# Transformer layer on one core: the MLP's norm factor stays in its PSUM bank and is applied in two portions, small evacuations are given priority, and the conv mixer's norm is spread over more steps

## The chip, the cores and the metric

The kernel runs on one core of a Trainium2 chip. The metric is the device time of one launch in microseconds; the median of the timed runs counts. A core has TensorE (PE, with its weight loads shown apart as PEld), VectorE (DVE), ScalarE (ACT), GpSimd (POOL) and the DMA queues, most of them issued here by SyncE (SP). Each engine works through its own instructions in the order in which the program puts them, and waits for others by semaphores.

## What is computed

One layer of a streaming encoder on x (2048 tokens, width 1024), all in float32:

```python
h = _rmsnorm(x, g_attn)
p = h @ w_in
y_a = a_b * _causal_dwconv(a_c * a_h, w_conv_a)
g = b_glu[..., :CONV_B_WIDTH] * jax.nn.sigmoid(b_glu[..., CONV_B_WIDTH:])
g = _causal_dwconv(g, w_conv_b) + b_conv_b
y_b = jax.nn.silu(_layernorm(g, ln_b_g, ln_b_b))
o = _stick_breaking(heads(q), heads(k), heads(v))
x = x + jnp.concatenate([y_a, y_b, y_c], axis=-1) @ w_out
h2 = _rmsnorm(x, g_ffn)
x = x + jnp.square(jax.nn.relu(h2 @ w_ff1)) @ w_ff2
```

`y_c` is o with its heads put side by side; a last RMS norm follows. The second convolution has 31 taps per channel, the attention has 8 heads of 64 and weighs a key by the product of the later keys' complements (no softmax), and the MLP has 4096 inner units.

## The kernel before

**Data.** Tokens lie along the free dimension in four blocks of 512 (`tb` = 0 to 3), channels on the 128 partitions, so a 128x512 tile is 128 channels of one block. Each factor of a large product is split into a high and a low part, and `mm3` (lines 100 to 108) does it as three passes of matmuls: high weights by high data (L103), low weights by high data (L105), high weights by low data (L107). The split of a tile is an ACT copy for the high part (L88) and a subtraction for the low one (L90, on DVE or POOL).

**Stages.** In the trace, the start and the input norms run to about 120 us; the input projection in two halves to about 512 us, each half with the conv mixer of two token blocks and, in the second half, the first round of the attention woven in; then come four blocks, which begin at about 512, 1000, 1500 and 2000 us. A block is the output projection, then the MLP, with the attention of the next token block woven in.

**The conv mixer** (`mixer_b`). For each token block and each of two channel groups, 31 DVE steps (L450, L452) add up the taps in a PSUM bank that bears the tag "c", of which there is one; an ACT copy takes the result to SBUF (`cb0`, `cb1`, L456). Then comes the LayerNorm over channels: the mean by two matmuls (L459, `ps_mean`, into the same single bank), its subtraction on DVE (L462), squares on ACT (L464), their sum on POOL (L467), a column sum on PE (L127, `ps_ss`), the reciprocal root (L115 on DVE, L118 on POOL), its spread over the partitions by PE (L134, `ps_R`), and the product. Each `yield` is a place where the weave can go over to other work; its number is a cost, and the number beside the mixer where it is woven in (83 and 98) is the cost that is spread over the half.

**The MLP of a block** (`block`). `acc0` to `acc7` hold the block's residual stream in SBUF. `ffn1(c)` makes 128 inner units in 24 matmuls, in two halves of 12; its bank `ps_u` goes through Relu and Square on ACT (L917, L918), is copied as high part `fh` (L926, ACT), and DVE subtracts for the low part `fl` (L927). After four such units `ffn2` multiplies them by the second weights into `ps_y`, and DVE adds that to acc (L952). After `ffn1(2)` the residual is multiplied by a factor of the norm: `mt` per token (L967), spread over the partitions by eight small matmuls into `ps_R` (L134), copied by ACT into an SBUF tile `ms` (L973), and then eight DVE multiplications acc = acc * ms (L975). The `z` banks (three in this stage) that `spread` takes from are also those of the attention's scores `ps_z` (L518, L519).

**The order of the work.** A scheduler puts each engine's instructions in order, by priorities that follow the order in which the program is written, and by a simulated time line. `high_priority(offset=HP)`, with HP = 200, moves the instructions inside it ahead by that many places in priority. The semaphores then keep that order on each engine.

Of the kernel before, what the change touches and what calls it, by code (L numbers as in the profile page):

```python
# [7 lines left out]
F32 = mybir.dt.float32  # L8
F32R = mybir.dt.float32r
# [6 lines left out]
P = 128  # L16
# [3 lines left out]
TB = 512  # L20
# [14 lines left out]
def f(ap):  # L35
    return ap.bitcast(F32)
# [32 lines left out]
class Trunk:  # L69
# [371 lines left out]
    def mixer_b(self, hf):  # L441
        nc = self.nc
        for tb in (2 * hf, 2 * hf + 1):
            acc = []
            for c in range(2):
                while (c, tb) not in self.g:
                    yield None
                g = self.g[c, tb]
                t = self.psum("ps_c", "c")
                nc.vector.tensor_scalar(t, g[:, 0:TB], self.wb[:, c, 0:1], self.vb["b_conv_b"][:, c : c + 1], op0=ALU.mult, op1=ALU.add)  # L450
                for k in range(1, 31):
                    nc.vector.scalar_tensor_tensor(t, g[:, k : k + TB], self.wb[:, c, k : k + 1], t, op0=ALU.mult, op1=ALU.add)  # L452
# [3 lines left out]
                nc.scalar.activation(acc[c], t, AF.Copy)  # L456
            mean = self.psum("ps_mean", "c")
            for c in range(2):
                nc.tensor.matmul(mean, self.avg, acc[c], start=c == 0, stop=c == 1)  # L459
            sqs = []  # L460
            for c in range(2):
                nc.vector.tensor_tensor(acc[c], acc[c], mean, op=ALU.subtract)  # L462
# [4 lines left out]
            nc.gpsimd.tensor_tensor(sqs[0], sqs[0], sqs[1], op=ALU.add)  # L467
            yv = self.rsqrt(self.colsum(sqs[:1], "c"), 1.0 / 256.0, LN_EPS)
            for _ in range(4):
                yield 1.8  # L470
            R = self.spread(yv, "c")
            for c in range(2):
                gg, bb = self.vb["ln_b_g"][:, c : c + 1], self.vb["ln_b_b"][:, c : c + 1]
                nc.vector.tensor_tensor(acc[c], acc[c], R, op=ALU.mult)
                s = self.mx.tile([P, TB], F32, name="sq", tag="sq", bufs=2)
                nc.scalar.activation(s, acc[c], AF.Sigmoid, bias=bb, scale=gg)
                nc.scalar.activation(acc[c], acc[c], AF.Identity, bias=bb, scale=gg)
                nc.gpsimd.tensor_tensor(s, acc[c], s, op=ALU.mult)

                nc.gpsimd.dma_start(self.Y[256 + c * P : 256 + (c + 1) * P, tb * TB : (tb + 1) * TB], s)  # L480
                yield 1.8
# [342 lines left out]
    def block(self, tb, before):  # L824
# [76 lines left out]
        def ffn1(*cs):  # L901

            for c in cs:
                need1(c)
            if len(cs) == 1:
                need1(cs[0] + 1)
            ws = [w1.pop(c) for c in cs]
            pus = [self.psum("ps_u", "d") for _ in cs]
            for q in range(2):
                for w, ps in zip(ws, pus):  # L910
                    self.mm3(ps, [(*w(d), hh[d], hl[d]) for d in range(4 * q, 4 * q + 4)], start=q == 0, stop=q == 1)
                    if q == 0:
                        yield 2.6
            if len(cs) > 1:
                need1(cs[-1] + 1)
            for c, ps in zip(cs, pus):
                nc.scalar.activation(ps, ps, AF.Relu)  # L917
                nc.scalar.activation(ps, ps, AF.Square)  # L918
                if tb == 3 and c > FC - G:

                    hi = self.at.tile([P, TB], F32R, name="fh", tag="Ahi", bufs=self.ab["Ahi"])
                    lo = self.at.tile([P, TB], F32R, name="fl", tag="Alo", bufs=self.ab["Alo"])
                else:
                    hi = hp.tile([P, TB], F32R, name="fh", tag="fh", bufs=G + 1)
                    lo = hp.tile([P, TB], F32R, name="fl", tag="fl", bufs=G + 1)
                nc.scalar.activation(hi, ps, AF.Copy)  # L926
                nc.vector.tensor_tensor(lo, ps, f(hi), op=ALU.subtract)  # L927
                fh[c], fl[c] = hi, lo
            yield 2.6 * len(cs)

        def ffn2(g, cols=slice(0, TB), ahead=0, again=0):

            cs = range(g * G, (g + 1) * G)

            def items(d):
                n = 4 * (g + again) + d // 2
                need2(n)
                t = w2[n]
                return [(t[:, 0, c % G, d % 2], t[:, 1, c % G, d % 2], fh[c][:, cols], fl[c][:, cols]) for c in cs]

            begun = []
            for d in range(ahead):
                begun.append(self.psum("ps_y", "d")[:, cols])
                self.mm3(begun[d], items(d)[:-1], stop=False)
            for d in range(DC):
                if d < ahead:
                    ps = begun[d]
                    self.mm3(ps, items(d)[-1:], start=False)
                else:
                    ps = self.psum("ps_y", "d")[:, cols]  # L950
                    self.mm3(ps, items(d))
                nc.vector.tensor_tensor(acc[d][:, cols], acc[d][:, cols], ps, op=ALU.add)  # L952
# [16 lines left out]
        nc.vector.scalar_tensor_tensor(em, mt, RMS_EPS, mt, op0=ALU.mult, op1=ALU.mult)  # L969
        yield from ffn1(2)  # L970
        need2(2)
        ms = hp.tile([P, TB], F32, name="ms", tag="ss", bufs=2)
        nc.scalar.activation(ms, self.spread(mt, "z"), AF.Copy)  # L973
        for d in range(DC):
            nc.vector.tensor_tensor(acc[d], acc[d], ms, op=ALU.mult)  # L975
        ss2 = hp.tile([P, TB], F32, name="ss2", tag="ss", bufs=2)
        sq7 = []
        for c in range(3, FC):
            yield from ffn1(c)
            if c < w2b:  # L980
                need2(c)
            if c % G == 0 and not (tb == 3 and c == FC - G):
                yield from ffn2(c // G - 1)
# [41 lines left out]
    def build(self):  # L1025
        tc = self.tc
        with ExitStack() as ctx:
# [6 lines left out]
            with ExitStack() as c1:  # L1034
                self.psum_pool(c1, d=3, c=1, z=2, q=1, o=1)
                self.p_pools(c1)
                self.w_eng = "dve"
                self.sb = 2
                self.xl = [[None] * DC for _ in range(2)]
                self.xh = [[None] * DC for _ in range(2)]  # L1040
                with tc.tile_pool(name="raw0", bufs=1) as self.rp:
                    self.rb, self.rt = 21, "raw"
                    self.p_start()
                self.rp = self.raw
                self.rb, self.rt = self.xb, "xt"
# [74 lines left out]
```

## Time and profile before

| | us |
|---|---|
| timed runs | 2442.66, 2449.86, 2449.74; median 2449.74 |
| profiled execution | 2452.1, of which the span is 2450.4 |
| mean granted TensorE clock, share of full speed | 0.992 |
| PE busy | 2390.6 |
| DVE busy | 1620.1 |
| POOL busy | 1161.3 |
| ACT busy | 1040.6 |

Times in the profile count from the start of the span; busy is the time in which an engine had an instruction in work. A row of a timeline gives start, duration, engine, line, operation, tiles and shape, a count if like instructions follow each other, and in brackets the idle time ahead of it with what ended it. PE's matmuls overlap, so a start-to-start distance says more of its pace than a duration.

### The profile page before, as it was taken

The page shows a single profiled execution, that of the slowest core. Times are in us where ns is not written, and L with a number is a line of the kernel's source. Part 1 is how long each engine was busy: PE and PEld are TensorE (multiplying, and loading weights), DVE is VectorE, ACT ScalarE, POOL GpSimd, SP SyncE. Part 2 cuts the span into 40 slices and gives each one's busy share as a digit, 9 for nine tenths or more (in the row PEclk, how much of TensorE's full clock was granted, in tenths as well). Part 3 has the DMA queues.
Part 4 walks back from the last instruction along what each step waited for, and adds up shares of the span by engine and source line. Part 5 has one row for each costly group of instructions (what it writes and reads, how often), then busy time and mean ns, then how long its engine had stood idle before and what let it go on. Part 6 is the DMA issues. An engine that isn't in the chain of part 4 may idle for free.

```text
span 2450.4 us, 32556 instructions
## 1 busy us (share of the span) xinstructions
PE 2390.6 (98%) x11316; PEld 2012.8 (82%) x11316; DVE 1620.1 (66%) x2380; ACT 1040.6 (42%) x1910; POOL 1161.3 (47%) x1221
## 2 busy tenths in 40 slices
PE   8999998999899999998999999999999999999998
PEld 7889877898788878887888888888888888888887
DVE  7957799943898977857777778577667735212114
ACT  5232532333466556534555555345555532121121
POOL 0342577641676666524676666168878720000000
PEclk9999999999999999999999999999999999999999
DMA  7569976779688777786877776876666556655555
GB/s 260 192 244 350 300 247 219 243 258 273 166 232 238 215 220 199 198 287 225 239 253 230 230 217 213 273 219 186 196 188 190 184 180 209 238 194 188 200 182 190
DMA packets 237061, 549.06 MB, mean 224 GB/s; under 512 B 26720, under 2 KB 100448, under 8 KB 218464
## 3 DMA queue, kind: packets, MB, share of 16 engines
q1 hardware_dynamic: 180304, 480.89, 58.1%
q0 software_dynamic: 37504, 56.64, 10.9%
q10 hardware_dynamic: 19088, 9.44, 1.3%
q8 instruction: 90, 1.47, 0.2%
q14 instruction: 75, 0.61, 0.1%
HBM read 390.38 MB, written 148.11 MB: 220 GB/s over the span
## 4 chain that ended last, share of the span: by engine, by line
PE 76%; DVE 15%; DMA 5%; issue 2%; POOL 1%; ACT 1%; SPq 0%; DVEq 0%; POOLq 0%; ACTq 0%
PE ps_y L107 8%; PE ps_y L103 8%; PE ps_y L105 8%; PE ps_u L103 7%; PE ps_u L105 7%; PE ps_u L107 7%; PE ps_p L105 4%; PE ps_p L107 4%; PE ps_p L103 4%; DVE A L659 2%; PE ps_x L103 2%; PE ps_z L518 2%; PE ps_x L105 2%; PE ps_x L107 2%; PE ps_z L519 2%
## 5 line engine op out<-in xcount | busy, mean ns | idle before, releaser
L90 POOL TENSOR_TENSOR Alo<-A,Ahi 128x512 fp32r<-128x512 f32 x288 | 395.1, 1383 | 104.2 <-PE ps_o L706 52.3
L952 DVE TENSOR_TENSOR acc<-acc,ps_y 128x512 f32<-128x512 f32 (+1 forms) x264 | 175.4, 667 | 195.6 <-PE ps_y L107 193.9
L107 PE MATMUL ps_y<-fl,w 128*128 128x512 f32 (+1 forms) x1056 | 279.8, 385 | 14.7 <-DVE fl L927 14.7
L103 PE MATMUL ps_u<-hh,w 128*128 128x512 f32 x1024 | 279.0, 393 | 6.2 <-DMA w<-s_w 6.2
L103 PE MATMUL ps_y<-fh,w 128*128 128x512 f32 (+1 forms) x1056 | 281.4, 386 | 2.5 <-DVE acc L952 1.3
L105 PE MATMUL ps_y<-fh,w 128*128 128x512 f32 (+1 forms) x1056 | 278.9, 384 | 0.0
L105 PE MATMUL ps_u<-hh,w 128*128 128x512 f32 x1024 | 275.0, 390 | 0.6 <-DVE w L90 0.6
L107 PE MATMUL ps_u<-hl,w 128*128 128x512 f32 x1024 | 275.0, 389 | 0.0
L601 POOL TENSOR_TENSOR A<-A,R 128x512 f32<-128x512 f32 x168 | 227.7, 1357 | 76.7 <-ACT A L599 54.6
L118 POOL TENSOR_TENSOR rs_y<-rs_v,mhalf 128x4 f32<-128x4 f32 (+1 forms) x13 | 14.7, 1131 | 523.3 <-DVE rs_v L117 486.1
L107 PEld LDWEIGHTS ps_y<-fl,w 128*128 128x128 f32 x1056 | 195.8, 189 | 55.9 <-DVE fl L927 17.0
L917 ACT ACTIVATE ps_u<-ps_u 128x512 f32<-128x512 f32 x128 | 74.8, 585 | 378.8 <-PE ps_u L107 378.5
L105 PEld LDWEIGHTS ps_y<-fh,w 128*128 128x128 f32 x1056 | 196.0, 189 | 40.2 <-DMA w<-wraw 0.4
L103 PEld LDWEIGHTS ps_y<-fh,w 128*128 128x128 f32 x1056 | 194.3, 189 | 40.7 <-DVE acc L952 2.1
L88 ACT ACTIVATE Ahi<-A 128x512 fp32r<-128x512 f32 x288 | 177.3, 627 | 118.4 <-PE ps_o L705 58.0
L105 PEld LDWEIGHTS ps_u<-hh,w 128*128 128x128 f32 x1024 | 192.1, 188 | 42.4 <-DVE w L90 1.5
L107 PEld LDWEIGHTS ps_u<-hl,w 128*128 128x128 f32 x1024 | 192.1, 188 | 40.1
L927 DVE TENSOR_TENSOR fl<-ps_u,fh 128x512 fp32r<-128x512 f32 x128 | 87.5, 685 | 207.1 <-ACT fh L926 206.6
L103 PEld LDWEIGHTS ps_u<-hh,w 128*128 128x128 f32 x1024 | 187.4, 189 | 42.5 <-DMA w<-s_w 6.4
L603 DVE TENSOR_TENSOR R<-ps_z,R 128x512 f32<-128x512 f32 x168 | 115.6, 688 | 126.4 <-ACT ps_z L600 93.8
L452 DVE SCALAR_TENSOR_TENSOR ps_c<-g,wb,ps_c 128x512 f32<-128x512 f32 x240 | 179.6, 748 | 4.6
L90 DVE TENSOR_TENSOR w<-wraw,w 128x512 fp32r<-128x512 f32 x152 | 150.4, 1007 | 24.1 <-ACT w L88 23.8
(175 smaller groups left out, 4881.2 us busy)
## 6 DMA issues: line engine op xcount, KB each, us to landing
w<-s_w SPq DMA_DIRECT2D x200, 512.0 KB, 3.4
w<-s_w SPq DMA_DIRECT2D x68, 1024.0 KB, 4.8
wraw<-in_w SPq DMA_DIRECT2D x192, 256.0 KB, 4.7
w<-s_w_out SPq DMA_DIRECT2D x64, 512.0 KB, 5.0
s_w<-w SPq DMA_DIRECT2D x32, 1024.0 KB, 5.4
s_w<-w SPq DMA_DIRECT2D x56, 512.0 KB, 4.4
Qd<-KQ SPq DMA_DIRECT2D x64, 256.0 KB, 6.4
xraw<-in_xT SPq DMA_DIRECT2D x48, 256.0 KB, 5.0
```

The source lines that it names most:

```text
L88: nc.scalar.activation(hi, x, AF.Copy)
L90: e.tensor_tensor(lo, x, f(hi), op=ALU.subtract)
L103: self.nc.tensor.matmul(ps, wh, xh, start=start and k == 0, stop=False)
L105: self.nc.tensor.matmul(ps, wl, xh, start=False, stop=False)
L107: self.nc.tensor.matmul(ps, wh, xl, start=False, stop=stop and k == n - 1)
L452: nc.vector.scalar_tensor_tensor(t, g[:, k : k + TB], self.wb[:, c, k : k + 1], t, op0=ALU.mult, op1=ALU.add)
L518: nc.tensor.matmul(z[:, oc], keys, g["qh"][:, qc], start=k == 0, stop=False)
L601: nc.gpsimd.tensor_tensor(t, t, R, op=ALU.mult)
L603: nc.vector.tensor_tensor(Rn, z, R, op=ALU.mult)
L917: nc.scalar.activation(ps, ps, AF.Relu)
L927: nc.vector.tensor_tensor(lo, ps, f(hi), op=ALU.subtract)
L952: nc.vector.tensor_tensor(acc[d][:, cols], acc[d][:, cols], ps, op=ALU.add)
```

## The change

It has four parts. The factor `ms` stays in the PSUM bank into which it was spread, with no ACT copy, and the eight multiplications read it from there. They are written in two portions of four with `ffn1(3)` between them. The evacuation of the inner units (Relu, Square, `fh`, `fl`) and the additions of `ps_y` to acc are put at high priority. And the mixer's norm is given three more yields ahead of the mean and two more ahead of the root, with larger costs for the weave (83 becomes 115, 98 becomes 116).

```diff
                 acc.append(self.mx.tile([P, TB], F32, name=f"cb{c}", tag="cb", bufs=2))
                 nc.scalar.activation(acc[c], t, AF.Copy)
+            for _ in range(3):
+                yield 1.8
             mean = self.psum("ps_mean", "c")
...
             yield 1.8
             nc.gpsimd.tensor_tensor(sqs[0], sqs[0], sqs[1], op=ALU.add)
+            for _ in range(2):
+                yield 1.8
             yv = self.rsqrt(self.colsum(sqs[:1], "c"), 1.0 / 256.0, LN_EPS)
...
-            for c, ps in zip(cs, pus):
-                nc.scalar.activation(ps, ps, AF.Relu)
-                nc.scalar.activation(ps, ps, AF.Square)
...
+            with self.tc.high_priority(offset=HP):
+                for c, ps in zip(cs, pus):
+                    nc.scalar.activation(ps, ps, AF.Relu)
+                    nc.scalar.activation(ps, ps, AF.Square)
...
+                    nc.scalar.activation(hi, ps, AF.Copy)
+                    nc.vector.tensor_tensor(lo, ps, f(hi), op=ALU.subtract)
+                    fh[c], fl[c] = hi, lo
...
-                nc.vector.tensor_tensor(acc[d][:, cols], acc[d][:, cols], ps, op=ALU.add)
+                with self.tc.high_priority(offset=HP):
+                    nc.vector.tensor_tensor(acc[d][:, cols], acc[d][:, cols], ps, op=ALU.add)
...
-        ms = hp.tile([P, TB], F32, name="ms", tag="ss", bufs=2)
-        nc.scalar.activation(ms, self.spread(mt, "z"), AF.Copy)
+        ms = self.spread(mt, "z")
         for d in range(DC):
+            if d == DC // 2:
+                yield from ffn1(3)
             nc.vector.tensor_tensor(acc[d], acc[d], ms, op=ALU.mult)
...
-        for c in range(3, FC):
+        for c in range(4, FC):
...
-                weave(self.p_half(0), [(Side(self.mixer_b(0)), 83, 20, 225, True), (Side(self.x_norms()), 24, 60, 180, True)])
+                weave(self.p_half(0), [(Side(self.mixer_b(0)), 115, 20, 225, True), (Side(self.x_norms()), 24, 60, 180, True)])
...
-                weave(self.p_half(1), [(Side(self.mixer_b(1)), 98, 0, 200, True), (a0, 28, 0, 210, True), (Side(self.pre_split()), len(self.presplit), 0, 200, True)])
+                weave(self.p_half(1), [(Side(self.mixer_b(1)), 116, 0, 200, True), (a0, 28, 0, 210, True), (Side(self.pre_split()), len(self.presplit), 0, 200, True)])
```

**What the scheduler makes of it.** A row below is one instruction: line, operation, output<-inputs and shape; a number behind a name tells one buffer from another of that name. Lines of the kernel after are 2 to 7 higher than those of the same code before (L975 is L982, L927 is L932, L459 is L461). SP's order is the same from the first block on, and PE's is the same from the middle of the second block on; in the third and fourth block only the ACT copy is gone.

DVE in the first block, before: the `fl` of one inner unit, the eight multiplications, a running sum of the attention (`R`), the low part of a first weight (`w1`), the next `fl`.

```order
L927 TENSOR_TENSOR fl_5993<-ps_u_5956,fh_5992 128x512
L975 TENSOR_TENSOR acc0_5546<-acc0_5546,ms_6015 128x512
L975 TENSOR_TENSOR acc1_5553<-acc1_5553,ms_6015 128x512
L975 TENSOR_TENSOR acc2_5562<-acc2_5562,ms_6015 128x512
L975 TENSOR_TENSOR acc3_5602<-acc3_5602,ms_6015 128x512
L975 TENSOR_TENSOR acc4_5642<-acc4_5642,ms_6015 128x512
L975 TENSOR_TENSOR acc5_5682<-acc5_5682,ms_6015 128x512
L975 TENSOR_TENSOR acc6_5722<-acc6_5722,ms_6015 128x512
L975 TENSOR_TENSOR acc7_5758<-acc7_5758,ms_6015 128x512
L603 TENSOR_TENSOR R_6063<-ps_z_6056,R_6003 128x512
L90 TENSOR_TENSOR w1_6132<-wraw_6133,w1_6132 128x512
L927 TENSOR_TENSOR fl_6080<-ps_u_6043,fh_6079 128x512
```

DVE at the same place, after:

```order
L932 TENSOR_TENSOR fl_5993<-ps_u_5956,fh_5992 128x512
L982 TENSOR_TENSOR acc0_5546<-acc0_5546,ps_R_6015 128x512
L982 TENSOR_TENSOR acc1_5553<-acc1_5553,ps_R_6015 128x512
L982 TENSOR_TENSOR acc2_5562<-acc2_5562,ps_R_6015 128x512
L982 TENSOR_TENSOR acc3_5602<-acc3_5602,ps_R_6015 128x512
L982 TENSOR_TENSOR acc4_5642<-acc4_5642,ps_R_6015 128x512
L982 TENSOR_TENSOR acc5_5682<-acc5_5682,ps_R_6015 128x512
L982 TENSOR_TENSOR acc6_5722<-acc6_5722,ps_R_6015 128x512
L982 TENSOR_TENSOR acc7_5758<-acc7_5758,ps_R_6015 128x512
L607 TENSOR_TENSOR R_6056<-ps_z_6049,R_6003 128x512
L90 TENSOR_TENSOR w1_6130<-wraw_6131,w1_6130 128x512
L932 TENSOR_TENSOR fl_6073<-ps_u_6036,fh_6072 128x512
```

The eight stand where they stood, all together and ahead of the next `fl`; what differs is that their second input is the bank `ps_R` in place of the SBUF tile.

DVE in the second block, before, with two instructions of the attention (`om` and its transpose `T`) among the multiplications:

```order
L927 TENSOR_TENSOR fl_10657<-ps_u_10584,fh_10656 128x512
L561 TENSOR_TENSOR om_10794<-om_10794 128x256
L975 TENSOR_TENSOR acc0_10334<-acc0_10334,ms_10816 128x512
L975 TENSOR_TENSOR acc1_10344<-acc1_10344,ms_10816 128x512
L975 TENSOR_TENSOR acc2_10356<-acc2_10356,ms_10816 128x512
L975 TENSOR_TENSOR acc3_10399<-acc3_10399,ms_10816 128x512
L975 TENSOR_TENSOR acc4_10442<-acc4_10442,ms_10816 128x512
L564 STREAM_TRANSPOSE T_10803<-om_10794 128x8x32
L975 TENSOR_TENSOR acc5_10485<-acc5_10485,ms_10816 128x512
L975 TENSOR_TENSOR acc6_10528<-acc6_10528,ms_10816 128x512
L975 TENSOR_TENSOR acc7_10567<-acc7_10567,ms_10816 128x512
L927 TENSOR_TENSOR fl_10663<-ps_u_10585,fh_10662 128x512
```

DVE there, after:

```order
L932 TENSOR_TENSOR fl_10655<-ps_u_10582,fh_10654 128x512
L982 TENSOR_TENSOR acc0_10332<-acc0_10332,ps_R_10814 128x512
L982 TENSOR_TENSOR acc1_10342<-acc1_10342,ps_R_10814 128x512
L982 TENSOR_TENSOR acc2_10354<-acc2_10354,ps_R_10814 128x512
L565 TENSOR_TENSOR om_10792<-om_10792 128x256
L982 TENSOR_TENSOR acc3_10397<-acc3_10397,ps_R_10814 128x512
L982 TENSOR_TENSOR acc4_10440<-acc4_10440,ps_R_10814 128x512
L982 TENSOR_TENSOR acc5_10483<-acc5_10483,ps_R_10814 128x512
L982 TENSOR_TENSOR acc6_10526<-acc6_10526,ps_R_10814 128x512
L982 TENSOR_TENSOR acc7_10565<-acc7_10565,ps_R_10814 128x512
L932 TENSOR_TENSOR fl_10661<-ps_u_10583,fh_10660 128x512
L568 STREAM_TRANSPOSE T_10801<-om_10792 128x8x32
```

Three multiplications come ahead of `om` and the other five follow each other; the next `fl` and then the transpose `T` stand behind the eighth.

PE in the second block, before, where attention scores (`ps_z`) and values (`ps_o`) stand ahead of the second half of an inner unit (the last row):

```order
L519 MATMUL ps_z_10977<-Qd_9716,Kl_10785 128x512
L518 MATMUL ps_z_11021<-Qd_9716,Kl_10785 128x512
L519 MATMUL ps_z_11021<-Qd_9716,Kl_10785 128x512
L705 MATMUL ps_o_10777<-Ahi_11031,Vl_10962 128x512
L706 MATMUL ps_o_10777<-Alo_11030,Vl_10962 128x512
L705 MATMUL ps_o_10777<-Ahi_11071,Vl_10962 128x512
L518 MATMUL ps_z_11061<-Qd_9716,Kl_10785 128x512
L519 MATMUL ps_z_11061<-Qd_9716,Kl_10785 128x512
L518 MATMUL ps_z_11091<-Qd_9716,Kl_10785 128x512
L519 MATMUL ps_z_11091<-Qd_9716,Kl_10785 128x512
L706 MATMUL ps_o_10777<-Alo_11070,Vl_10962 128x512
L103 MATMUL ps_u_10724<-hh_10444,w1_10652 128x512
```

PE there, after:

```order
L522 MATMUL ps_z_10973<-Qd_9714,Kl_10783 128x512
L523 MATMUL ps_z_10973<-Qd_9714,Kl_10783 128x512
L709 MATMUL ps_o_10775<-Ahi_11027,Vl_10958 128x512
L710 MATMUL ps_o_10775<-Alo_11026,Vl_10958 128x512
L709 MATMUL ps_o_10775<-Ahi_11067,Vl_10958 128x512
L522 MATMUL ps_z_11017<-Qd_9714,Kl_10783 128x512
L523 MATMUL ps_z_11017<-Qd_9714,Kl_10783 128x512
L710 MATMUL ps_o_10775<-Alo_11066,Vl_10958 128x512
L103 MATMUL ps_u_10722<-hh_10442,w1_10650 128x512
```

Two pairs of scores (those of `ps_z` 11061 and 11091 before) have gone behind that half unit, and of the pairs that stay one now comes last.

PE in the second projection half, where the mixer's mean for the third token block (`ps_mean`) stands within a projection unit, before:

```order
L107 MATMUL ps_p_3547<-xl0_2_2275,wh15_3286 128x512
L107 MATMUL ps_p_3547<-xl0_3_2281,wh15_3286 128x512
L107 MATMUL ps_p_3547<-xl0_4_2287,wh15_3286 128x512
L107 MATMUL ps_p_3547<-xl0_5_2293,wh15_3286 128x512
L459 MATMUL ps_mean_3441<-cb0_3004,avg_76 128x512
L459 MATMUL ps_mean_3441<-cb1_3439,avg_76 128x512
L107 MATMUL ps_p_3547<-xl0_6_2299,wh15_3286 128x512
L107 MATMUL ps_p_3547<-xl0_7_2305,wh15_3286 128x512
```

PE there, after (the three matmuls ahead are the first pass of the same unit):

```order
L103 MATMUL ps_p_3547<-xh0_0_2300,wh15_3297 128x512
L103 MATMUL ps_p_3547<-xh0_1_2306,wh15_3297 128x512
L103 MATMUL ps_p_3547<-xh0_2_2312,wh15_3297 128x512
L461 MATMUL ps_mean_3401<-cb0_2900,avg_76 128x512
L461 MATMUL ps_mean_3401<-cb1_3278,avg_76 128x512
L103 MATMUL ps_p_3547<-xh0_3_2318,wh15_3297 128x512
L103 MATMUL ps_p_3547<-xh0_4_2324,wh15_3297 128x512
L103 MATMUL ps_p_3547<-xh0_5_2330,wh15_3297 128x512
```

The mean stands behind the third matmul of the unit where it stood behind the twenty-second: 18 rows of the program earlier. The column sum for this block (L127) is 16 rows earlier, and the mean for the fourth token block 28 rows earlier. On DVE the two subtractions of this mean (L462) stood behind all three small steps L625 of an attention scan and five instructions more; now they stand behind the first L625. In the first half the means of the two blocks stand earlier as well.

More of the change, by code (lines that the diff above doesn't have):

```diff
@@ L915, in ffn1 @@
                 need1(cs[-1] + 1)
-            for c, ps in zip(cs, pus):
-                nc.scalar.activation(ps, ps, AF.Relu)
-                nc.scalar.activation(ps, ps, AF.Square)
[L919 to L928, printed above, removed]
+            with self.tc.high_priority(offset=HP):
+                for c, ps in zip(cs, pus):
+                    nc.scalar.activation(ps, ps, AF.Relu)
+                    nc.scalar.activation(ps, ps, AF.Square)
+                    if tb == 3 and c > FC - G:
+                        hi = self.at.tile([P, TB], F32R, name="fh", tag="Ahi", bufs=self.ab["Ahi"])
+                        lo = self.at.tile([P, TB], F32R, name="fl", tag="Alo", bufs=self.ab["Alo"])
+                    else:
+                        hi = hp.tile([P, TB], F32R, name="fh", tag="fh", bufs=G + 1)
+                        lo = hp.tile([P, TB], F32R, name="fl", tag="fl", bufs=G + 1)
+                    nc.scalar.activation(hi, ps, AF.Copy)
+                    nc.vector.tensor_tensor(lo, ps, f(hi), op=ALU.subtract)
+                    fh[c], fl[c] = hi, lo
             yield 2.6 * len(cs)
```

## Prediction

> **What bounds the kernel now.** I read the page first, then the waits of PE, then the stretches in which PE stood, and in those the rows of the engine that PE waited for. The first two lines of the page:
>
> ```profile
> span 2450.4 us, 32556 instructions
> ...
> PE 2390.6 (98%) x11316; PEld 2012.8 (82%) x11316; DVE 1620.1 (66%) x2380; ACT 1040.6 (42%) x1910; POOL 1161.3 (47%) x1221
> ```
>
> PE is busy for 98% of the span, and the change takes no matmul away. So it can win only what PE loses by standing, and the time after it in which PE runs at a reduced clock. PE's waits that the change touches (total, times, longest):
>
> ```profile
> PE ps_y L107 <- DVE fl L927: 14.7, 6, 7.4
> ...
> PE ps_z L518 <- ACT A L533: 5.9, 1, 5.9
> PE ps_mean L459 <- ACT cb L456: 4.1, 1, 4.1
> PE ps_ss L127 <- POOL sq L467: 3.1, 1, 3.1
> ...
> PE ps_y L103 <- DVE acc L952: 1.3, 2, 1.0
> ```
>
> The 7.4 us stand in the first block, the 5.9 us in the second, the mean and its column sum in the second projection half. The granted clock in stretches behind such waits (duration, PE, PEld, DVE, ACT, POOL, clock, DMA, GB/s):
>
> ```profile
> 640.00:660.00 20.00, 13.80 (x56) 11.34 (x57) 19.77 (x31) 8.05 (x15) 10.64 (x13) 0.83 0.37 99
> 380.00:401.00 21.00, 17.93 (x66) 14.28 (x65) 17.97 (x21) 5.10 (x10) 17.83 (x18) 0.77 0.69 248
> ```
>
> The clock is under 1 there, so a wait costs more than itself.
>
> **First block.** DVE's eight multiplications by `ms` in the four blocks (line L975 alone: length, busy time), and DVE operations by form:
>
> ```profile
> 630.00:646.00 16.00, 12.27 (x8) 0.89 0.55 140
> 1104.00:1119.00 15.00, 11.25 (x8) 0.82 0.90 295
> 1600.00:1608.00 8.00, 4.97 (x8) 1.00 0.58 188
> 2095.00:2103.00 8.00, 4.91 (x8) 1.00 0.63 228
> ```
>
> ```profile
> L952 DVE TENSOR_TENSOR acc<-acc,ps_y 128x512 f32<-128x512 f32 x248 | 168.8, 683 | 191.3 <-PE ps_y L107 190.1
> L90 DVE TENSOR_TENSOR w<-wraw,w 128x512 fp32r<-128x512 f32 x152 | 150.4, 1007 | 24.1 <-ACT w L88 23.8
> ```
>
> The same eight take 12.27 and 11.25 us in two blocks and 4.97 and 4.91 in the others. What differs is POOL beside them. In the timeline of the first block:
>
> ```profile
> 632.08 12.27 DVE L975 TENSOR_TENSOR acc<-acc,ms 128x512 f32<-128x512 f32 x8
> 632.16 1.32 POOL L90 TENSOR_TENSOR Alo<-A,Ahi 128x512 fp32r<-128x512 f32 x1
> ...
> 642.06 1.13 POOL L571 TENSOR_TENSOR A<-A,om 128x256 f32<-128x256 f32 x1
> ...
> 644.27 0.68 DVE L603 TENSOR_TENSOR R<-ps_z,R 128x512 f32<-128x512 f32 x1
> 644.87 0.68 DVE L90 TENSOR_TENSOR w<-wraw,w 128x512 fp32r<-128x512 f32 x1
> 645.47 0.68 DVE L927 TENSOR_TENSOR fl<-ps_u,fh 128x512 fp32r<-128x512 f32 x1
> ...
> 646.20 0.79 PE L107 MATMUL ps_y<-fl,w 128*128 128x512 f32 x1 [7.36 <-DVE fl L927]
> 646.79 1.91 PE L103 MATMUL ps_y<-fh,w 128*128 128x512 f32 x4
> 648.50 1.45 PE L105 MATMUL ps_y<-fh,w 128*128 128x512 f32 x4
> 649.78 1.07 PE L107 MATMUL ps_y<-fl,w 128*128 128x512 f32 x4
> ```
>
> POOL works from 632.16 to 643.2, and DVE operations with two SBUF inputs, as the multiplication and L90's split (1007 ns on average), are drawn out beside it. L952 adds a PSUM bank to the same acc tiles, in all stages, and stays at 683 ns; in a row such operations follow each other by 0.60 us (644.27, 644.87, 645.47). With `ps_R` from PSUM the eight are of L952's kind: 8 x 0.60 = 4.8, about the 4.97 of the third block. From 632.08 they end at 637.0, R at 637.6; then L90's split runs beside POOL, from 0.6 to the 1.5 us or so that one multiplication took there (12.27/8), and `fl` is ready at 638.9 to 639.8 where it was at 646.15. PE stood from 646.20 - 7.36 = 638.84, so it waits 0.1 to 1.0, and 6.4 to 7.3 are gained, 6.8 in the middle. Behind the wait PE is slow: from the four L103 to the four L105 it takes 1.71 us, from those to L107 1.28, from the first matmul to the L103 0.59. At full pace a matmul follows in 0.23 (1.07 for four, of which the last overlaps what comes next, is 0.92), so these nine lose 0.8 + 0.4 + 0.3 = 1.5, and that goes with the wait. Sum 8.3, from 7.0 to 8.8.
>
> [...]
>
> The written portions do nothing here: the order keeps all eight ahead of `fl`. The wait of 1.0 us for acc L952, at 668, goes with the earlier sums: 1, from 0 to 1.
>
> **Second block.** DVE, PE and the weights:
>
> ```profile
> 1104.97 1.36 DVE L561 TENSOR_TENSOR om<-om 128x256 f32<-128x256 f32 x1
> 1106.25 8.98 DVE L975 TENSOR_TENSOR acc<-acc,ms 128x512 f32<-128x512 f32 x5
> 1115.15 0.43 DVE L564 STREAM_TRANSPOSE T<-om 128x256 f32<-128x256 f32 x1
> 1116.82 0.81 PE L518 MATMUL ps_z<-Qd,Kl 128*128 128x512 f32 x1 [5.88 <-ACT A L533]
> 1119.27 1.57 PE L103 MATMUL ps_u<-hh,w 128*128 128x512 f32 x4
> ```
>
> ```profile
> 1102.30 1.23 SPq L79 DMA_DIRECT2D w<-s_w  x2
> ```
>
> ```profile
> w<-s_w SPq DMA_DIRECT2D x1, 512.0 KB, 11.1
> ```
>
> Today `T` waits behind five drawn-out multiplications, the ACT copies and the bank behind `T`, and PE behind the bank from 1110.94. After, three multiplications run from 1104.97 to 1106.8, `om` (two SBUF inputs) for 0.4 to 4 us, five more for 3.0: acc7 is done by 1111.2 if `om` takes its 1.36, by 1113.8 at worst. This now matters to PE: its last pair of scores needs the bank that `ps_R` holds until acc7 has read it. `fl`, `T` and two ACT copies follow by 1113 to 1116 and release only pairs that now come later. What is late next is a weight: issued at 1102.30, it lands 11.1 later, at 1113.4, and the half unit that started at 1119.27 needs it. So the half unit starts 5.9 earlier, less the two pairs put behind it (four matmuls, 0.9): 5.0, and 0.5 for its first four matmuls (1.57 against 1.07). With `om` at its worst 4, with a slow weight 3: 5, from 3 to 6.
>
> **Mixer.** For the third token block:
>
> ```profile
> 373.01 4.70 DVE L452 SCALAR_TENSOR_TENSOR ps_c<-g,wb,ps_c 128x512 f32<-128x512 f32 x6
> ...
> 380.89 5.65 DVE L625 TENSOR_TENSOR C<-C,T 32x16 f32<-32x16 f32 x3
> ...
> 389.35 1.28 DVE L462 TENSOR_TENSOR cb<-cb,ps_mean 128x512 f32<-128x512 f32 x2
> ```
>
> ```profile
> 378.39 1.12 PE L459 MATMUL ps_mean<-cb,avg 128*128 128x512 f32 x2 [4.08 <-ACT cb L456]
> ...
> 393.61 1.87 PE L127 MATMUL ps_ss<-ones,sq 128*128 128x2 f32 x8 [3.07 <-POOL sq L467]
> ...
> 395.92 3.62 PE L105 MATMUL ps_p<-xh,wl 128*128 128x512 f32 x8
> ```
>
> PE reaches the mean at 374.3 and stands 4.08. After, it stands 18 rows, 4.1 us, earlier (0.23 each), at 370.2. In DVE's order four steps of the convolution fewer are then left, 4 x 0.78 = 3.1, so it ends some 3 us earlier: the wait is about 5, 1 more than now, anywhere from 0 to 9 as DVE's drawn-out operations fall. Behind it I expect a gain: the subtractions (389.35) no longer stand behind the three L625 (5.65 us) and five more, so POOL's sum comes some 5 earlier, the column sum's 3.07 goes, and with it half of the 3.62 us of eight L105 (1.8). 3.1 + 1.8 - 1 = 4, from -4 to 8.
>
> The mean and the second group's copy for the fourth block:
>
> ```profile
> 493.19 1.88 PE L459 MATMUL ps_mean<-cb,avg 128*128 128x512 f32 x4
> ```
>
> ```profile
> 483.29 0.60 ACT L456 ACTIVATE cb<-ps_c 128x512 f32<-128x512 f32 x1 [3.11 <-DVE ps_c L452]
> ```
>
> The mean moves 28 rows (6.4 us) ahead, to 486.8; the copy is done at 483.9, which covers it by 2.9 us; the two means of the first half move too, and their convolution with them. Nothing: 0, if a cover goes up to -3.
>
> Third and fourth block, where the multiplications take 4.97 and 4.91 already: 0. The other high priorities leave PE's order alone. Sum: 8.3 + 1 + 5 + 4 = 18.3 off the profiled execution's 2452.1 gives 2433.8; that execution lies 2.4 over the median of 2449.74, so I forecast 2432.
>
> **The rivals.** *The wait is taken over (no difference).* In the first block L90's split stays between acc7 and `fl`; if POOL holds it until 643.2, `fl` comes at 643.9 and 5 of 7.36 us stay, with the slow matmuls behind: gain 2.3. In the second block the weights, whose queue is at a 0.90 share in that stretch, come as late as PE does now: 1 to 3. With the mixer at 0 that is 4 to 6, so 2444. For it: the split's mean of 1007 ns. Against it: only one such operation is left where there were nine. 0.16.
>
> *The mean is met too early (slower).* PE works in order, and all projection matmuls stand behind the mean. If DVE's convolution ends as late as today, the third block's mean waits 4.1 longer and the column sum, moved by 16 rows, 3.6 longer, each with another 1.8 of slow matmuls: 11.3. If the fourth block's 28 rows also meet an unfinished convolution, that is 6.4 - 2.9 + 1.8 = 5.3, and as much in the first half: 21.9 lost. It decides once it is over the blocks' 14.3; all of it gives 7.6 more than now, 2457. For it: DVE is the engine that PE waits for here, and the six steps at 373.01 run without a gap (4.70 us for six), so there is no slack to end earlier in. Against it: DVE's order moves the same steps ahead. 0.07.
>
> *The change doesn't do what it says.* As far as the portions go, this is so and priced above. If `ps_R` in PSUM were as slow as `ms`, only the acc sum's 1 and the mixer's 4 would be left, 2445; L952's 683 ns speaks against it. It is within the first rival's chance.
>
> **How the numbers follow.** About 0.3%, 7 us, is what a measurement can tell from no change: 2442.4 and less is faster, 2457 and more slower. Forecast 0.77, taken over 0.16, too early 0.07. The terms' best ends, 8.8 + 1 + 6 + 8 = 23.8, give 2426; below them the lowest timed run, 2442.66, lay 7 under the median, so I go 4 further, to 2422. The upper end takes in the first rival: 2445.
>
> **What would show it.** Right: the eight multiplications take about 5 us in every block; PE's wait for `fl` in the first block is under 1.5 us; the wait for ACT's A in the second is gone, with 2 to 4 us for a weight or acc in its place; the column sum's wait is gone. Wrong: multiplications over 0.8 us each, a wait of 4 us or more for `fl` after L90, or a wait at a mean of over 6 us.

## The result and the profile after

The changed kernel takes 2438.36 us in the median of 10 runs (2431.60 to 2442.65), the kernel before 2449.80 (10 runs, 2442.66 to 2459.73). The ratio is 0.9949, with a 95% interval from 0.9931 to 0.9967: 11.4 us less, where the prediction said 17.7 (2432). The profiled executions lie 13.5 us apart (2452.1 and 2438.63). The first lines of the page of the kernel after:

```profile
span 2436.9 us, 32569 instructions
...
PE 2389.6 (98%) x11316; PEld 2011.6 (83%) x11316; DVE 1607.1 (66%) x2380; ACT 1038.2 (43%) x1906; POOL 1152.2 (47%) x1221
```

PE has the same 11316 matmuls and is as busy as it was; what is gone is time in which it stood. Its waits, total, times and longest:

```profile
PE ps_y L107 <- DVE fl L932: 6.7, 5, 2.3
PE ps_u L103 <- DMA w<-s_w: 6.6, 7, 1.8
...
PE ps_mean L461 <- ACT cb L456: 4.0, 1, 4.0
PE ps_p L103 <- DVE u L355: 3.8, 1, 3.8
...
PE ps_y L103 <- DVE acc L958: 2.5, 3, 1.7
```

The 7.4 us for `fl` and the 5.9 us for the scores' bank have gone, and so has the column sum's 3.1. New are 3.8 us for `u` (L355, a step of the first conv mixer) where there were 1.2, and the waits for acc have grown (1.3 to 2.5).

Since PE's matmuls are the same in number and nearly in order, the start of a matmul of the same place in both traces shows where the time went. The numbers count the matmuls of a trace; the differences are between the two profiled executions.

| stretch, by PE's matmuls | before, us | after, us | difference |
|---|---|---|---|
| start to 3100 (up to the multiplications of the first block) | 617.48 | 618.67 | +1.2 |
| 3100 to 3240 (the multiplications of the first block) | 36.70 | 27.70 | -9.0 |
| 3240 to 4120 (rest of the first block) | 191.73 | 193.32 | +1.6 |
| 4120 to 5240 (up to the multiplications of the second block) | 252.17 | 251.37 | -0.8 |
| 5240 to 5400 (the multiplications of the second block) | 43.52 | 38.27 | -5.3 |
| 5400 to 11300 (to the end) | 1297.62 | 1296.69 | -0.9 |

So the gain lies where the eight multiplications of the first two blocks stand: 14.3 us. That is no accident of these two executions. In the traces of all the runs below that have the eight multiplications by an SBUF tile (five, the kernel before among them), the stretch of the first block takes 36.3 to 38.4 us and that of the second 43.5 to 45.4; in those with a PSUM bank (seven, the changed kernel among them; the last two experiments, which alter the attention, are left out), 27.7 to 28.7 and 36.2 to 41.9. The rest of the first block takes 191.4 to 192.5 in the five and 192.8 to 195.0 in the seven, so there some of the gain is always lost again.

Those multiplications alone, in the first, third and fourth block (length of the window, DVE's busy time in them, clock, DMA share, GB/s):

```profile
621.00:641.00 20.00, 4.85 (x8) 1.00 0.61 187
...
1588.00:1600.00 12.00, 4.86 (x8) 1.00 0.68 216
2080.00:2095.00 15.00, 4.87 (x8) 1.00 0.70 263
```

They took 12.27 in the first block and take 4.85 now, as in the blocks where nothing disturbed them before. The timeline of the first block, DVE and then POOL and PE:

```profile
632.41 4.85 DVE L982 TENSOR_TENSOR acc<-acc,ps_R 128x512 f32<-128x512 f32 x8
637.19 0.67 DVE L607 TENSOR_TENSOR R<-ps_z,R 128x512 f32<-128x512 f32 x1
637.79 1.04 DVE L90 TENSOR_TENSOR w<-wraw,w 128x512 fp32r<-128x512 f32 x1
638.76 0.68 DVE L932 TENSOR_TENSOR fl<-ps_u,fh 128x512 fp32r<-128x512 f32 x1
```

```profile
635.02 1.32 POOL L90 TENSOR_TENSOR Alo<-A,Ahi 128x512 fp32r<-128x512 f32 x1
```

```profile
639.86 0.40 PE L107 MATMUL ps_y<-fl,w 128*128 128x512 f32 x1
640.09 1.07 PE L103 MATMUL ps_y<-fh,w 128*128 128x512 f32 x4
```

POOL works beside them as before. `fl` is ready at 639.44, the matmul that needs it runs with no wait at all, and the four behind it take 1.07 us where they took 1.91. The L90 split, whose two inputs are both in SBUF, was still drawn out, to 1.04 us (in the trace of before it took 0.68 there, with GpSimd done).

The second block, DVE, PE, and the weight of the half unit with its time from issue to landing:

```profile
1098.34 1.87 DVE L982 TENSOR_TENSOR acc<-acc,ps_R 128x512 f32<-128x512 f32 x3
1100.13 1.89 DVE L565 TENSOR_TENSOR om<-om 128x256 f32<-128x256 f32 x1
1101.94 3.06 DVE L982 TENSOR_TENSOR acc<-acc,ps_R 128x512 f32<-128x512 f32 x5
```

```profile
1105.06 0.62 PE L522 MATMUL ps_z<-Qd,Kl 128*128 128x512 f32 x1
1105.52 0.40 PE L523 MATMUL ps_z<-Qd,Kl 128*128 128x512 f32 x1
1105.76 0.39 PE L710 MATMUL ps_o<-Alo,Vl 128*128 128x512 f32 x1
1106.42 1.20 PE L103 MATMUL ps_u<-hh,w 128*128 128x512 f32 x4 [0.27 <-DMA w<-s_w]
```

```profile
1095.20 1.69 SPq L79 DMA_DIRECT2D w<-s_w  x2
```

```profile
w<-s_w SPq DMA_DIRECT2D x1, 512.0 KB, 11.2
```

The eighth multiplication ends at 1105.0 and the last pair of scores starts at 1105.06, in the bank that it frees, with no wait that the view shows. The weight issued at 1095.20 lands at 1106.4, and the half unit starts at 1106.42, after 0.27 us of waiting for it. The weight is what comes last, and the bank came free just in time.

### The profile page after: what moved, and what is told of

Its sections match the earlier page's. It is cut to its first block, busy times and chain, and to the rows that moved or that the text cites. A ratio compares the mean times of both kernels' runs of the same rounds, so it can differ in the third digit from the quotient of the medians.

```text
span 2436.9 us, 32569 instructions
## 1 busy us (share of the span) xinstructions
PE 2389.6 (98%) x11316; PEld 2011.6 (83%) x11316; DVE 1607.1 (66%) x2380; ACT 1038.2 (43%) x1906; POOL 1152.2 (47%) x1221
## 3 DMA queue, kind: packets, MB, share of 16 engines
q0 software_dynamic: 37504, 56.64, 11.1%
## 4 chain that ended last, share of the span: by engine, by line
PE 77%; DVE 13%; DMA 5%; issue 2%; ACT 1%; POOL 1%; SPq 0%; DVEq 0%; POOLq 0%; ACTq 0%
PE ps_y L107 8%; PE ps_y L103 8%; PE ps_y L105 8%; PE ps_u L103 7%; PE ps_u L105 7%; PE ps_u L107 7%; PE ps_p L107 4%; PE ps_p L103 4%; PE ps_p L105 4%; PE ps_x L103 2%; PE ps_x L105 2%; PE ps_x L107 2%; PE ps_z L522 2%; DMA w<-s_w 2%; PE ps_z L523 2%
## 5 line engine op out<-in xcount | busy, mean ns | idle before, releaser
L90 POOL TENSOR_TENSOR Alo<-A,Ahi 128x512 fp32r<-128x512 f32 x288 | 394.8, 1381 | 111.9 <-PE ps_o L710 53.8
L958 DVE TENSOR_TENSOR acc<-acc,ps_y 128x512 f32<-128x512 f32 (+1 forms) x264 | 175.4, 667 | 194.7 <-PE ps_y L107 192.8
L103 PE MATMUL ps_y<-fh,w 128*128 128x512 f32 (+1 forms) x1056 | 281.1, 386 | 4.5 <-DVE acc L958 2.5
L103 PE MATMUL ps_u<-hh,w 128*128 128x512 f32 x1024 | 278.8, 393 | 6.6 <-DMA w<-s_w 6.6
L103 PEld LDWEIGHTS ps_y<-fh,w 128*128 128x128 f32 x1056 | 193.6, 189 | 43.4 <-DVE acc L958 3.6
L105 PEld LDWEIGHTS ps_u<-hh,w 128*128 128x128 f32 x1024 | 192.8, 188 | 41.1
L932 DVE TENSOR_TENSOR fl<-ps_u,fh 128x512 fp32r<-128x512 f32 x128 | 87.5, 684 | 209.9 <-ACT fh L931 209.4
L103 PEld LDWEIGHTS ps_u<-hh,w 128*128 128x128 f32 x1024 | 186.8, 188 | 43.0 <-DMA w<-s_w 9.2
L88 ACT ACTIVATE w<-wraw 128x512 fp32r<-128x512 f32 x152 | 91.9, 628 | 183.7 <-PE ps_y L107 114.8
```

Source lines behind the costliest of these rows:

```text
L88: nc.scalar.activation(hi, x, AF.Copy)
L90: e.tensor_tensor(lo, x, f(hi), op=ALU.subtract)
L103: self.nc.tensor.matmul(ps, wh, xh, start=start and k == 0, stop=False)
L105: self.nc.tensor.matmul(ps, wl, xh, start=False, stop=False)
```

## The experiments

Each is timed beside the kernel before on one chip; a ratio is to that kernel.

**One edit: the factor stays in PSUM.**

```diff
-        ms = hp.tile([P, TB], F32, name="ms", tag="ss", bufs=2)
-        nc.scalar.activation(ms, self.spread(mt, "z"), AF.Copy)
+        ms = self.spread(mt, "z")
```

> The kernel before with one edit: the factor stays in its PSUM bank. Theory (the gain comes from the source of the multiplications, PSUM in place of SBUF): all eight take 4.8 to 5.0 us in every block, the wait of 7.4 us for fl in the first block falls under 1.5, the wait of 5.9 us for the scores' bank in the second goes, and the ratio to before is 0.994 to 0.996, as for the whole change. Rival A (the priorities make the gain): 0.999 to 1.001. Rival B (the mixer's steps make a part of it): the ratio stays 1 to 3 us short of the whole change's.

2441.96 us, ratio 0.9966 (0.9950 to 0.9982). The first two blocks' multiplications, by their line alone:

```profile
618.00:642.00 24.00, 4.85 (x8) 1.00 0.64 187
1086.00:1112.00 26.00, 4.94 (x8) 0.93 1.06 343
```

Both waits are gone, and the stretches of the table are 28.2 and 36.2 us (8.5 and 7.3 less). PE's order in the blocks is that of the whole change: all the moved rows there come from this edit. So this edit by itself brings the gain of the blocks. The ratio, 8.8 us in the medians, is a little outside of what was expected, and 3.6 us short of the whole change's median, which leaves rival B open; the intervals of the two overlap.

**The whole change but for this edit.**

```diff
-        ms = self.spread(mt, "z")
+        ms = hp.tile([P, TB], F32, name="ms", tag="ss", bufs=2)
+        nc.scalar.activation(ms, self.spread(mt, "z"), AF.Copy)
```

> The changed kernel with the copy into SBUF put back, all else of the change kept. Theory: the multiplications in the first two blocks take 11 to 12.5 us again, the two waits come back, ratio to before 0.999 to 1.001. Rival A (priorities): the gain stays, 0.994 to 0.996.

2446.68 us, 0.9986 (0.9971 to 1.0000). The multiplications in the first two blocks:

```profile
630.00:650.00 20.00, 12.30 (x8) 0.83 0.52 142
1100.00:1122.00 22.00, 10.99 (x8) 0.84 0.79 253
```

They are slow again, and waits of 6.6 us for `fl` and 5.2 for the scores' bank are back. Rival A falls: priorities and portions don't make the gain of the blocks. The ratio is a little lower than was expected; this kernel still has the mixer's part, which is taken up below.

**The priorities alone** (Relu, Square, `fh`, `fl` and the sums of acc inside `high_priority`, nothing else).

> The kernel before with the high priorities alone. Theory: the multiplications as before, the 7.4 and 5.9 us waits as before, ratio 0.9995 to 1.0005. Rival A: 0.994 to 0.997.

2453.43 us, 1.0005 (0.9989 to 1.0021). PE's and POOL's order is that of before row for row, DVE's differs only in a few rows near 1810 us, and the waits are 7.5 us for `fl` and 6.7 for the bank. The multiplications are as slow as before:

```profile
630.00:655.00 25.00, 12.30 (x8) 0.86 0.51 142
1104.00:1130.00 26.00, 12.51 (x8) 0.80 0.71 231
```

The priorities do nothing that can be measured.

**The copy kept, but into PSUM.** This takes apart two things that the change does at once: it spares an ACT copy, and it puts the operand into another memory.

```diff
-        ms = hp.tile([P, TB], F32, name="ms", tag="ss", bufs=2)
+        ms = self.psum("ms", "z")
         nc.scalar.activation(ms, self.spread(mt, "z"), AF.Copy)
```

> The kernel before with the ACT copy kept, but made into a second PSUM bank in place of an SBUF tile. Theory (what counts is where the second input lies): the multiplications take 4.8 to 5.0 us in all four blocks although the copy is still there; the wait for fl in the first block under 2 us; ratio 0.994 to 0.998, where a second bank of the scores held for some us may cost up to 4 us. Rival C (the missing ACT copy and its wait are what helps): multiplications of 11 to 12 us in the first two blocks, 0.999 to 1.001.

2443.18 us, 0.9966 (0.9946 to 0.9986). The multiplications, in the four blocks:

```profile
618.00:640.00 22.00, 4.86 (x8) 1.00 0.61 163
1086.00:1112.00 26.00, 4.91 (x8) 0.93 0.83 264
1580.00:1600.00 20.00, 4.87 (x8) 1.00 0.80 196
2070.00:2095.00 25.00, 4.87 (x8) 0.93 0.66 247
```

With the copy still there, the ratio is that of the bank without it (0.9966). It is the operand's place that counts; rival C falls.

**GpSimd work beside the multiplications of the fourth block**, where GpSimd had none; the products go nowhere. Once in the kernel before, once in the changed one, each executed once, so that only the profile counts here.

```diff
+        if tb == 3:
+            dm = self.at.tile([P, TB], F32, name="dm", tag="A0", bufs=self.ab["A0"])
+            nc.gpsimd.tensor_tensor(dm[:, 0:4], mt, mt, op=ALU.mult)
+            for _ in range(14):
+                nc.gpsimd.tensor_tensor(dm, f(hh[0]), f(hh[1]), op=ALU.mult)
```

> The kernel before with 14 added products of two SBUF tiles on GpSimd in the fourth block, around the eight multiplications by the SBUF copy; their result is not used. GpSimd has no other work there. Theory (two SBUF inputs on DVE are drawn out beside GpSimd): the eight multiplications of the fourth block take 9 to 16 us where they took 4.91. Rival D (the first two blocks are slow for another reason, such as DMA): they stay at 4.9 to 5.1.

> The changed kernel with the same 14 added products on GpSimd in the fourth block. Theory: the eight multiplications from PSUM stay at 4.8 to 5.0 us beside them. Rival D: as slow or as fast as in the kernel before with the same addition.

The eight multiplications and POOL's work beside them, from the SBUF copy:

```profile
2100.22 13.52 DVE L980 TENSOR_TENSOR acc<-acc,ms 128x512 f32<-128x512 f32 x8 [1.68 <-ACT ms L978]
```

```profile
2098.70 17.56 POOL L976 TENSOR_TENSOR dm<-hh 128x512 f32<-128x512 f32 x11
```

And from the PSUM bank:

```profile
2081.21 4.87 DVE L987 TENSOR_TENSOR acc<-acc,ps_R 128x512 f32<-128x512 f32 x8 [1.05 <-PE ps_R L134]
```

```profile
2080.32 19.07 POOL L982 TENSOR_TENSOR dm<-hh 128x512 f32<-128x512 f32 x14
```

13.52 us against 4.87 with the same added work beside them, at a place where 4.91 were needed before. That is the effect by itself, as far as this case shows it: beside GpSimd's products the eight of two SBUF tiles on DVE were drawn out, the eight of an SBUF tile and a PSUM bank were not. Rival D falls.

**The mixer's part alone, and the whole change without it.**

```diff
+            for _ in range(3):
+                yield 1.8
             mean = self.psum("ps_mean", "c")
...
+            for _ in range(2):
+                yield 1.8
             yv = self.rsqrt(self.colsum(sqs[:1], "c"), 1.0 / 256.0, LN_EPS)
```

(with 83 made 115 and 98 made 116; the second kernel is the changed one with all of this undone)

> The kernel before with the mixer's added yields and larger costs alone. Theory (in the mixer a wait for u takes the place of the column sum's): a wait of 3 to 4 us for DVE's u ahead of the third block's mean, one of about 4 at the mean, none at its column sum; ratio 0.999 to 1.001. Rival B (the mixer's steps bring the 4 us that the prediction gave them): 0.998 or less, with the wait for u a matter of this one execution.

> The changed kernel without the mixer's part. Theory: the same as the whole change within 1.5 us, ratio 0.994 to 0.996, with the waits at the mean (4.1) and the column sum (3.1) as before. Rival B: 0.996 to 0.998.

Alone 2448.50 us, 0.9991 (0.9977 to 1.0004). The change without it 2440.83, 0.9966 (0.9951 to 0.9982), which is where rival B expected it (0.996 to 0.998) and not the theory; that profile has a wait of 3.7 us in the second block which tells of the other bound:

```profile
1099.69 3.51 DVE L561 TENSOR_TENSOR om<-om 128x256 f32<-128x256 f32 x1
1103.12 3.06 DVE L978 TENSOR_TENSOR acc<-acc,ps_R 128x512 f32<-128x512 f32 x5
```

```profile
1106.24 0.82 PE L518 MATMUL ps_z<-Qd,Kl 128*128 128x512 f32 x1 [3.73 <-DVE acc L978]
```

Here `om` between the multiplications was held for 3.51 us, and PE's next pair of scores waits for the bank that the factor still holds. In the changed kernel's profile the same instruction took 1.89.

In the second projection half the traces say what the mixer's part does. The product om x R of the attention (L584; L580 before) and the wait for `u`, changed kernel:

```profile
345.25 6.18 DVE L584 TENSOR_TENSOR om<-om,R 128x256 f32<-128x256 f32 x1
...
349.87 1.27 POOL L90 TENSOR_TENSOR wpl<-wraw,wph 128x512 fp32r<-128x512 f32 x1
...
359.14 0.67 DVE L355 TENSOR_TENSOR u<-ps_p,ac 128x512 f32<-128x512 f32 x1
```

```profile
359.87 3.78 PE L103 MATMUL ps_p<-xh,wh 128*128 128x512 f32 x8 [3.80 <-DVE u L355]
379.60 3.78 PE L461 MATMUL ps_mean<-cb,avg 128*128 128x512 f32 x4 [4.02 <-ACT cb L456]
```

The same product in the kernel before, with the last of POOL's instructions beside it:

```profile
343.60 5.02 DVE L580 TENSOR_TENSOR om<-om,R 128x256 f32<-128x256 f32 x1
...
347.05 1.28 POOL L90 TENSOR_TENSOR wpl<-wraw,wph 128x512 fp32r<-128x512 f32 x1
```

In DVE's new order the product of two SBUF tiles L584 meets a longer run of POOL's work: POOL's last run of instructions beside it, one straight behind the other, goes from 344.94 to 351.14 (from 343.30 to 348.33 before), and the product ends 0.3 us after that run both times. In the five profiled executions with the mixer's part in this form it takes 6.2 us each time, and the wait for `u` is 3.8 to 5.4; in the seven without it, 3.5 to 5.0 and 0.6 to 2.2. The wait at the column sum is then gone, which is 1.2 to 3.1 without. The whole stage ends at the same time: matmul 2300 starts at 482.1 to 483.3 us in the five (mean 482.8) and at 478.6 to 486.7 in the seven (mean 483.0).

**The whole change and the one without the mixer's part, once more, on one chip.**

> The changed kernel once more, unaltered, on the same chip as the three others of this call, to compare them with it: 0.993 to 0.997. Both theories expect the wait for DVE's u (3 to 5.5 us) and none at the column sum.

> The changed kernel without the mixer's part once more, beside the whole change on one chip. Theory (the mixer's part moves a wait and wins nothing): within 2 us of the whole change. Rival B (it wins what the prediction gave it): 3 to 5 us slower than the whole change.

2436.46 us, 0.9943 (0.9924 to 0.9961), and 2442.56, 0.9956 (0.9938 to 0.9973). Here the whole change has the lower median by 6.1 us, and by 2.5 against the first run without the mixer's part, which was not timed beside it; both times the intervals overlap. The theory had said within 2 us. Alone, the mixer's part was 2.3 us under the kernel before, so all the medians lean towards a gain. The traces show none at the end of the stage, but each is one execution: that of this second run without the mixer's part was 6.4 us faster than its own median (2436.18), those of the whole change within 0.3 of theirs. Whether the mixer's part wins a few microseconds, and where, stays open.

**The same reasoning carried on: om x R on GpSimd.**

```diff
-        nc.vector.tensor_tensor(om[:, hi2], om[:, hi2], R[:, hi2], op=ALU.mult)
+        nc.gpsimd.tensor_tensor(om[:, hi2], om[:, hi2], R[:, hi2], op=ALU.mult)
```

> The changed kernel with one more edit by the same reasoning: the product om x R of the attention's diagonal part (L584, two SBUF inputs, up to 6.2 us on DVE) is made by GpSimd. Theory (drawn-out DVE products set the waits of PE in the second projection half): the wait for DVE's u (3.8 us) goes, the one at the third block's mean falls from 4.0 to under 2, ratio to before 0.991 to 0.994. Rival E (GpSimd takes the place of DVE as what is late): new waits behind GpSimd's Alo or the transpose, ratio 0.995 to 0.998.

2434.10 us, 0.9929 (0.9911 to 0.9946). PE's waits:

```profile
PE ps_o L701 <- ACT Ahi L88: 6.8, 3, 3.5
...
PE ps_y L103 <- DVE fl L932: 4.8, 4, 1.9
PE ps_y L103 <- DVE acc L958: 2.9, 1, 2.9
...
PE ps_mean L461 <- ACT cb L456: 0.7, 1, 0.7
```

The wait for `u` is gone and that at the mean is 0.7; matmul 2300 starts at 476.66, 6.3 us earlier than in the changed kernel's profile. At matmul 11300 it is 4.2 us ahead of the first profile of the changed kernel (2421.86 and 2426.02) and 1.9 of the second (2423.76), and the timed medians lie 2.4 apart, with intervals that overlap: by these figures a third to two thirds are given back in the blocks. The rest of the first block alone takes 196.6 us where it took 193.3, with the wait of 2.9 for acc in it. The waits for a high part that ACT copies stand in the projection half itself, at 304, 343 and 371 us, so that the 6.3 us are what is left after them. Both theories have a share; that the added edit makes the kernel faster is not shown.

With the product before it (L582) on GpSimd too:

> As the run with om x R on GpSimd, and the product before it (om x R into R, L582) on GpSimd too. Theory: as there or 1 to 2 us better, 0.990 to 0.994. Rival E: worse than there, 0.996 to 1.000.

2432.62 us, 0.9924 (0.9907 to 0.9941): the lowest median of all, 18.6 us under the kernel before on its chip, and not to be told from the run before it. The wait for `fl` rises to 10.0 and 7.6 us in two groups, and the second projection half ends 11.0 us earlier than in the changed kernel (matmul 2300 at 471.99), most of which is given back. Against the changed kernel on the same chip (0.9943) the intervals overlap.

## Why the prediction was right, and where its sum was off

**First block.** Predicted 8.3 us (7.0 to 8.8), with `fl` at 638.9 to 639.8 and a wait of 0.1 to 1.0 left. Measured 9.0, just over that range, with `fl` at 639.44 as forecast and no wait left, because PE came a microsecond later than the step assumed: the whole wait of 7.36 went, and the 1.5 of slow matmuls behind it. The kind of operation that L952 is (683 ns in the mean of all stages, 691 at most) was the right row to go by: 4.85 us for eight against the 4.8 worked out. The low clock behind the wait went with it (0.83 from 640 to 660 us before, 1.00 now). The lower end of the range, 7.0, does not follow from the step's own terms, which give 6.4 + 1.5 = 7.9.

Reading the factor from PSUM cost DVE nothing that shows here: with GpSimd idle beside them the fourth block's eight take 4.87 us and took 4.91 from SBUF; the third block's take 4.86 (0.89 us of GpSimd's work beside them) and took 4.97 (0.19 us). With GpSimd's added products beside them in the fourth block it is 4.87 for one SBUF input and 13.52 for two.

**Second block.** Predicted 5 (3 to 6), measured 5.3. The step that the weight comes last held: issue to landing was 11.2 us against the 11.1 used, and the half unit started as it landed. That PE would wait 2 to 4 us there did not: the wait was 0.27, since PE came later, at a low clock (0.83 from 1094 to 1104 us) behind the weight wait ahead (1.79 us). The bank that `ps_R` holds, named as what matters to PE, came free within 0.1 us of PE's need here and cost 3.7 us in one experiment. That the term came out within 0.3 us is in part luck: against the 43.5 us of before, the seven traces with a PSUM bank show gains from 1.6 to 7.3 in this stretch.

**Sums of acc.** Predicted 1 (0 to 1); the step failed. The wait of 1.0 did not go, it grew to 1.74:

```profile
661.57 1.19 PE L103 MATMUL ps_y<-fh,w 128*128 128x512 f32 x4 [1.74 <-DVE acc L958]
```

```profile
645.70:663.00 17.30, 15.21 (x66) 11.96 (x65) 16.94 (x27) 7.37 (x14) 12.51 (x13) 1.00 0.49 115
```

DVE (the third busy time) works 16.94 of 17.30 us there. PE reached this place about 7 us earlier than before, DVE's chain of the attention only as fast as it always was, and one place in the order is 0.6 us. The wait comes with the bank: at this place it is 1.4 to 1.8 in all seven traces with a PSUM bank, the two with that edit alone included, and the run with priorities alone has no gain. I take it, with the lower pace behind it, for the main part of the 1.6 us given back in the rest of the block; that is argued, and no run tested it alone.

**Mixer.** Predicted 4 (-4 to 8); in the traces 0.2 on the mean of five and seven executions, and -0.3 in the two compared here (482.68 and 482.98). By the traces this term makes most of the amount by which the sum was too large; by the timed medians, which lean to 2.3 to 6.1 us, it may well be right. Two steps of it held: the wait at the mean stayed (4.02, where about 5 was said) and the column sum's wait went. What failed in the traces is the sum "3.1 + 1.8 - 1 = 4": it holds the waits that the trace of before shows, and no new one. The convolution steps that moved ahead pushed `u` back and put L584 beside a longer run of POOL's work, and the slow matmuls went along (eight L103 in 3.78 us behind that wait). The prediction named DVE's drawn-out operations only as the range of the mean's wait.

**The sum.** In the medians it was 17.7 and 11.4 came. What the runs show of the difference is the acc term, 1 forecast and 1.6 lost in its stage. The edit of the bank alone is worth 8.8 us in the medians (4.4 to 12.3 by its interval), where the prediction's terms for it add up to 14.3 and its own trace has 15.8 in the two stretches, less 3.3 lost in the rest of the first block. How the remainder of the difference falls on the bank, the mixer and the spread between executions stays open.

**The rivals.** The wait that is taken over came in part: the wait for `u` stands in the place of the column sum's, so that the second projection half ends 0.3 us later, and 1.6 us are lost behind the first block's multiplications, where the wait for acc stands; L90's split, which the rival had named, was held for 1.04 us only. The mean met too early did not come; the wait there was the same, and the covers of the other three means held (no wait at them). That the written portions do nothing, as the order showed, fits the run with everything but the bank, 0.9986.

## What to carry to other kernels

Where the same DVE instruction takes twice as long in one stage as in another (here 12.27 us for eight against 4.97), look at GpSimd's row beside it, and at how many of the instruction's inputs lie in SBUF (13.52 us with two beside GpSimd's products, 4.87 with one). An operand that is in a PSUM bank already, and is read a few times (eight here, 8.8 us less by that edit alone), may be better left there than copied, if no one needs the bank meanwhile: count who comes next for it (PE waited 3.73 us for the bank in one run). When a wait is taken away, the next one is found by asking which engine has no idle time in the stretch behind it, and not by the waits that the old trace shows.

## What the runs showed that was not expected

How hard a single DVE product is held: om x R, 128x256, takes 0.42 us with POOL idle beside it (at 379.88 in the changed kernel) and 6.2 beside POOL's work, at the same place in all five executions with the mixer's part. The order alone does not settle it: without that part, with the instructions of PE, DVE, POOL and ACT in one and the same order up to there, it took 5.0 us in five executions and 3.5 in the two of the changed kernel without the mixer's part. The eight in the fourth block took 13.52 us for 4.9 of work, while the first 11 of the added GpSimd products of 128x512 took 17.56, 1.6 each; the added products with the PSUM form took 1.36 each (19.07 for 14), so GpSimd's were 0.23 us slower each where DVE's were drawn out.

The place where the second half of the projection ends varied over 8.2 us between executions of the same order of instructions there (seven profiles), and over 1.2 in the other order (five).
